# SSD mixer: an even tile's diagonal matmuls queued behind its odd neighbour's, its carried matmuls in one run in another PSUM bank, and a warm-up on a constant

## The chip, the cores and the metric

One core of a Trainium2 chip runs the kernel. A core has five engines with queues of their own: TensorE (PE in the profile; PEld is its loading of the stationary operand, which overlaps with matmuls), VectorE (DVE), ScalarE (ACT), GpSimd (POOL) and SyncE (SP, which here only issues DMAs). Each engine takes its instructions in the order in which they were written into its queue, and waits on semaphores of the others. Matmuls write to PSUM, which has eight banks of 512 fp32 numbers per partition; all else lies in SBUF.

The metric is the time of one execution on the device, in microseconds. Before: a median of 1420.25 over 3 runs (1419.76 to 1420.65).

## The reference

Two layers over 512 tokens of width 1024. Layer 0 mixes tokens with a Mamba-2 SSD, layer 1 with HGRN2; after each comes a squared-ReLU MLP, with layer norms around, and a gated embedding. The change is in layer 0's mixer, at the very start of the kernel, and in one line of layer 1. The SSD cuts the 512 tokens into four chunks of 128, and computes for each head:

```python
cb = jnp.einsum('bclgn,bcsgn->bcgls', cm, bm)
y_diag = jnp.einsum('bcgls,bcgrls,bcsgrp->bclgrp', cb, decay, xdt)
states = jnp.einsum('bclgn,bclgr,bclgrp->bcgrpn', bm, decay_to_end, xdt)
# prev: the states, carried from chunk to chunk with the chunk's decay
y_off = jnp.einsum('bclgn,bcgrpn,bclgr->bclgrp', cm, prev, jnp.exp(a_cs))
y = y_diag + y_off + d_skip * xs        # then times silu(z), an RMS norm, and w_out
```

`y_diag` is what a chunk takes from itself (the diagonal part), `y_off` what it takes from the chunks before (the carried part).

## The kernel before

**Matmuls.** A projection in fp32 is made of three fast matmuls: each operand is split into a high and a low part (`whi`/`wlo` for weights, `b8` for activations), and `mm3` (lines 120 to 122) adds high by high, high by low and low by high into one bank. A weight unit is loaded by SP (`raw`, line 106), its high part is cut by ACT (line 113), and its low part by DVE (line 116). These matmuls are 512 columns wide, and nearly all of the kernel's time. The SSD's small products (lines 676, 703, 715, 745, 751, 777) are plain fp32 matmuls of 128 or 64 columns. The profile counts such an fp32 matmul as two passes, so three of them show as x6, and eight as x16.

**The SSD's loop.** Sixteen tiles of 128 channels (two heads of 64) pass one after another. In step `j` the loop projects tile `j` (`xz`: 48 fast matmuls for x and z, a convolution on DVE, line 644), and works on tile `i = j - 1` in `core`. Per tile, `core` does this:

- four transposes of xs into the bank `pt` (line 703); DVE makes from it `xw` and `xdt` (lines 710 and 711);
- the states: three matmuls into the bank `pm` (line 715), from which DVE forms the carried states `pv` in five instructions (lines 722 to 725), each of which needs the one before;
- the decay matrix `m`, on DVE and ACT (lines 731 to 735);
- the diagonal part: eight matmuls (line 745) whose stationary operand, a head's slice of `xdt`, is 64 columns wide. They write the two halves of the bank `py0`, one head to each;
- the carried part: three matmuls (line 751) into the bank `py1`, one for each of chunks 1 to 3, each with another of the three carried states as an operand;
- the sum of these, in the DVE lines 758 to 761, and then the scaled and split result in `ys` (lines 810 and 811) and its squares (line 766).

After every fourth tile an RMS norm is due (`rms_group`: 16 passes, line 777, whose stationary operand is 64 columns wide as well), and a quarter of the output projection.

**What sets the order.** The kernel's text is not the order on the engines. A scheduler takes the instructions by their dependences, by a priority, and by its own estimates of durations, and writes a fixed order for each engine. `tc.high_priority(offset=n)` moves a block forward in that order, and `behind(ins)` makes a block's instructions on one engine stand after `ins`. The scheduler fills the time between the small products of `core` with the fast matmuls of the next tile's projection. In layer 1's mixer PE's order is written by hand (line 1143); DVE's is still the scheduler's.

**The start.** DVE clears a tile with zeros (line 151), and PE multiplies it four times with itself (line 154) while the first DMAs are on their way; the result is used nowhere. Then come the first projections (lines 593 and 120 to 122), whose operands wait for DMAs (line 162) and for the splits behind them (lines 168 to 173).

**In layer 1**, `out0` (line 899) is a part of the output projection that runs between the small products of the last heads; its result is added to `acc` by DVE (line 911). The same stretch has DVE instructions on the path of PE's small products: lines 965 and 966 write `qd`, which line 991's matmuls read, first for one head and then for the other.

Of the kernel before, what the change touches and what calls it, by code (L numbers as in the profile page):

```python
# [8 lines left out]
F32 = mybir.dt.float32  # L9
# [6 lines left out]
P = 128  # L16
# [28 lines left out]
def trunk(ctx: ExitStack, tc, a):  # L45
# [27 lines left out]

    two = dict(xs=2, sz=2, cv=2, cm=2, cbm=2)
    mlp = dict(r=8, blk=2, sg=2)
    bufs = dict(ssd=dict(two, ss=2), mlp0=mlp, hgrn=dict(two, xs=4, sz=4, cv=4, y=2, pv=2, btok=2, sc=2, scb=2, qd=2), mlp1=mlp)
    phase = []

    def begin(name):
# [67 lines left out]
    acc = mk(accp, [P, NCH, D], "acc")  # L147

    with tc.high_priority(offset=FIRST):
        idle = tmp("sq", [P, T])  # L150
        nc.vector.memset(idle, 0.0)
        ps = bank(psm, "pm")
        for _ in range(4):
            nc.tensor.matmul(ps[:, :256], idle[:, :P], idle[:, :256], start=True, stop=True)  # L154

    x_s = Split(8)
    four = [(mk(whip, [P, 2, T], "whi", F32R), mk(wlop, [P, 2, T], "wlo", F32R)) for _ in range(4)]
# [535 lines left out]
        nc.scalar.activation(sz, ps, AF.Silu)  # L693
        return xs, sz

    def core(j, xs, sz, y, toks, btok, cbm, cm, ss=None):
# [41 lines left out]
        for r in range(2):  # L738
            rs = slice(64 * r, 64 * r + 64)
            nc.scalar.activation(ecs[rs], csb[rs, r, P:], AF.Exp)  # L740
        yd = bank(psy, "py0")
        for c in range(NCH):
            sl = slice(c * P, (c + 1) * P)
            for r in range(2):
                nc.tensor.matmul(  # L745
                    yd[64 * r : 64 * r + 64, sl], xdt[:, 2 * c + r, :], m[:, r, sl], start=True, stop=True
                )
        ri = None if ss is None else rms_group(ss)
        yo = bank(psy, "py1")
        for c in range(1, NCH):  # L750
            nc.tensor.matmul(  # L751
                yo[:, c * P : (c + 1) * P],
                pv[:, c - 1].rearrange("p h q -> p (h q)"),
                cm[:, c * P : (c + 1) * P],
                start=True,
                stop=True,
            )
        nc.vector.scalar_tensor_tensor(y, xs, dskip[:, j : j + 1], yd, ALU.mult, ALU.add)
# [13 lines left out]
    def rms_group(ss):  # L772

        pr = bank(pst, "pt")
        for c in range(NCH):
            for r in range(0, P, 64):
                nc.tensor.matmul(
                    pr[r : r + 64, 64 * c : 64 * c + 64], ss[:, c * P + r : c * P + r + 64], ones_s, start=True, stop=True
                )
# [6 lines left out]
        out_project(a["wso"][4 * g : 4 * g + 4], s, False, *after, scale=ri)  # L786

    pend = None
    ys = None
    bcm = None  # L790
    prep = None
    outs = []
    for j in range(17):
        nbcm = bc_group(j // 4) if j % 4 == 0 and j < 16 else None
        cur = xz(j) if j < 16 else None
        if j == 4:
            nc.sync.dma_start(acc, a["x"])
            for c in range(NCH):
                nc.vector.tensor_scalar(acc[:, c, :], acc[:, c, :], ALPHA, None, ALU.mult)
        if pend is not None:  # L800
            i = j - 1
            if i % 4 == 0:
                ys = Split(4)
                ss = None
                prep = bc_prep(bcm)
            y = tmp("y", [P, T])
            due = bool(outs) and (i % 4 == 1 or i == 15) and i != 13
            ri = core(i, *pend, y, toks, *prep, outs[0][2] if due else None)
            w = snw[:, i : i + 1]
            nc.scalar.activation(ys.h(i % 4), y, AF.Copy, scale=w)  # L810
            nc.vector.scalar_tensor_tensor(ys.l(i % 4), y, w, f32(ys.h(i % 4)), ALU.mult, ALU.subtract)
            ss = sq_sum(y, ss)
# [86 lines left out]
    def out0():  # L899
        for h in range(2):  # L900
            units = [unit(a["who"][2 * h + i]) for i in range(2)]
            for c in range(NCH):
                sl = slice(c * P, (c + 1) * P)
                ps = bank(psj, "pj")
                for k in range(4):
                    hi, lo = units[k // 2]
                    ks = slice((k % 2) * 512, (k % 2 + 1) * 512)
                    mm3(ps, halves[0].h(k, sl), halves[0].l(k, sl), hi[:, ks], lo[:, ks], k == 0, k == 3)
                    yield 0.65
                d = acc[:, c, h * 512 : (h + 1) * 512]  # L910
                nc.vector.scalar_tensor_tensor(d, d, ALPHA, ps, ALU.mult, ALU.add)

    def background():
        yield from qf(0)
# [365 lines left out]
```

## Time and profile before

| | |
|---|---|
| median of 3 runs | 1420.25 us (1419.76 to 1420.65) |
| the profiled execution | 1420.26 us, its span 1418.5 us |
| around the span | 1.76 us |
| DVE, ACT busy | 1057.1 us (75%), 754.1 us (53%) |
| the SSD with its output projection | about the first 390 us of the span |
| layer 1's mixer | about 770 to 1040 us |

The span is one profiled execution from its first to its last instruction. In the timeline a row has its start, its duration, the engine, the line, the operation, output and inputs, and a count of instructions that were merged into it. Matmuls overlap, and their ends are modelled, so what one costs is read from the starts of the rows around it, and not from its duration. In the lists of waits a row has the engine and line that waited, what it waited for, the total, the number of times and the longest.

### The profile page before, as it was taken

Reading aid. Unit: us, or ns where it says so; the run is one execution under the profiler, and the core shown is the slowest. Engines: PE = TensorE matmul, PEld = TensorE weight load, DVE = VectorE, ACT = ScalarE, POOL = GpSimd, SP = SyncE. Lnnn points to the kernel's source line nnn. Section 1 sums busy time; section 2 is a strip of 40 time slices with the busy share of each in tenths; the row PEclk is TensorE's granted clock in tenths of the full one; section 3 lists DMA queues with packets and bytes.
Section 4 is the critical chain, followed back from the end, with each engine's and each line's share of the span. In section 5 each row is a group of like instructions: output and inputs, shape, how many; then the busy total and the mean of one; then the engine's idle time right before and its main releaser. Section 6 shows DMA issues by size and latency. Waiting matters only on the chain.

```text
span 1418.5 us, 20411 instructions
## 1 busy us (share of the span) xinstructions
PE 1412.0 (100%) x8061; PEld 1174.1 (83%) x8061; DVE 1057.1 (75%) x1760; ACT 754.1 (53%) x1134; POOL 1.9 (0%) x12
## 2 busy tenths in 40 slices
PE   9999999999999999999999999999999999999998
PEld 7888888888888888888888888887898888888887
DVE  7988687787877667677986577678785867667873
ACT  6776455563265454545555547655555544544641
POOL 0000000000000000000000000000000000000000
PEclk9999999999999999999999999999999999999999
DMA  8432323223333434344521321222063444434231
GB/s 304 138 129 95 119 90 119 104 101 122 150 133 122 155 130 155 132 154 163 208 90 49 134 90 61 76 91 91 33 250 104 149 148 135 149 134 164 90 119 45
DMA packets 49391, 178.02 MB, mean 126 GB/s; under 512 B 5520, under 2 KB 6288, under 8 KB 49168
## 3 DMA queue, kind: packets, MB, share of 16 engines
q1 hardware_dynamic: 49296, 176.73, 35.8%
q8 instruction: 63, 1.03, 0.3%
q14 instruction: 32, 0.26, 0.1%
HBM read 174.54 MB, written 2.16 MB: 125 GB/s over the span
## 4 chain that ended last, share of the span: by engine, by line
PE 98%; ACT 1%; DVE 1%; issue 0%; DVEq 0%; ACTq 0%
PE pj L120 25%; PE pj L121 25%; PE pj L122 24%; PE py L120 5%; PE py L122 5%; PE py L121 5%; PE py L745 1%; PE pt L239 1%; PE py L751 1%; PE pm L715 1%; PE py L991 1%; PE pt L703 1%; PE py L1117 0%; PE py L1119 0%; PE py L1056 0%; PE pm L154 0%
## 5 line engine op out<-in xcount | busy, mean ns | idle before, releaser
L113 ACT CAST whi<-raw 128x1024 fp32r<-128x1024 f32 x222 | 232.9, 1052 | 326.4 <-PE pj L121 233.1
L120 PE MATMUL pj<-b,whi 128*128 128x512 f32 (+1 forms) x1006 | 383.0, 381 | 0.0
L121 PE MATMUL pj<-b,whi 128*128 128x512 f32 (+1 forms) x1006 | 380.4, 378 | 0.0
L122 PE MATMUL pj<-b,wlo 128*128 128x512 f32 (+1 forms) x1006 | 379.9, 378 | 0.0
L116 DVE TENSOR_TENSOR wlo<-raw,whi 128x1024 fp32r<-128x1024 f32 x222 | 269.6, 1220 | 137.2 <-ACT whi L113 132.6
L120 PEld LDWEIGHTS pj<-b,whi 128*128 128x128 f32 x1006 | 189.4, 188 | 33.5 <-issue 0.3
L122 PEld LDWEIGHTS pj<-b,wlo 128*128 128x128 f32 x1006 | 189.3, 188 | 33.4
L121 PEld LDWEIGHTS pj<-b,whi 128*128 128x128 f32 x1006 | 189.4, 188 | 33.1 <-issue 0.9
L122 PE MATMUL pj<-whi,b 128*128 128x512 f32 x544 | 213.6, 393 | 0.0
L120 PE MATMUL pj<-whi,b 128*128 128x512 f32 x536 | 213.0, 397 | 0.0
L121 PE MATMUL pj<-wlo,b 128*128 128x512 f32 x536 | 210.3, 392 | 0.0
L122 PEld LDWEIGHTS pj<-whi,b 128*128 128x128 f32 x544 | 102.2, 188 | 20.9
L120 PEld LDWEIGHTS pj<-whi,b 128*128 128x128 f32 x536 | 100.8, 188 | 20.2 <-ACT b L1138 0.3
L121 PEld LDWEIGHTS pj<-wlo,b 128*128 128x128 f32 x536 | 100.8, 188 | 19.5
L113 ACT CAST whi<-r 128x1024 fp32r<-128x1024 f32 x72 | 75.7, 1053 | 67.7 <-PE pj L122 38.6
L116 DVE TENSOR_TENSOR wlo<-r,whi 128x1024 fp32r<-128x1024 f32 x72 | 87.6, 1219 | 23.8 <-ACT whi L113 23.2
L122 PE MATMUL py<-whi,b 128*128 128x512 f32 (+1 forms) x250 | 97.0, 388 | 0.0
L121 PE MATMUL py<-wlo,b 128*128 128x512 f32 x224 | 87.2, 389 | 0.0
L120 PE MATMUL py<-whi,b 128*128 128x512 f32 x224 | 87.1, 390 | 0.0
L122 PEld LDWEIGHTS py<-whi,b 128*128 128x128 f32 x250 | 46.9, 188 | 9.6
L644 DVE SCALAR_TENSOR_TENSOR cv<-pj,cst,cv 128x509 f32<-128x509 f32 (+2 forms) x66 | 48.6, 744 | 3.5 <-ACT cv L641 2.8
L120 PEld LDWEIGHTS py<-whi,b 128*128 128x128 f32 x224 | 42.0, 188 | 9.2 <-DVE sg L504 0.3
(310 smaller groups left out, 1864.3 us busy)
## 6 DMA issues: line engine op xcount, KB each, us to landing
raw<-in_w SPq DMA_DIRECT2D x112, 512.0 KB, 3.3
r<-in_w SPq DMA_DIRECT2D x64, 512.0 KB, 3.4
raw<-in_wssd SPq DMA_DIRECT2D x36, 512.0 KB, 3.4
a<-csd SPq DMA_DIRECT2D x16, 512.0 KB, 3.7
raw<-in_wso SPq DMA_DIRECT2D x16, 512.0 KB, 3.2
raw<-in_wg SPq DMA_DIRECT2D x16, 512.0 KB, 3.5
raw<-in_whq SPq DMA_DIRECT2D x16, 512.0 KB, 3.3
raw<-in_whvg SPq DMA_DIRECT2D x14, 512.0 KB, 3.3
```

What stands on the lines that cost most here:

```text
L113: nc.scalar.copy(hi[:, :n], f)
L116: nc.vector.tensor_sub(lo[:, :n], f, f32(hi[:, :n]))
L120: nc.tensor.matmul(out, sh, mh, start=start, stop=False, **kw)
L121: nc.tensor.matmul(out, sh, ml, start=False, stop=False, **kw)
L122: nc.tensor.matmul(out, sl, mh, start=False, stop=stop, **kw)
L239: nc.tensor.transpose(pt[:, j * P : (j + 1) * P], src[:, k * P : (k + 1) * P], ident)
L644: nc.vector.scalar_tensor_tensor(cv[:, d:], ps[:, : T - d], convw[:, i, k : k + 1], cv[:, d:], ALU.mult, ALU.add)
L703: nc.tensor.transpose(pt[:, c * P : (c + 1) * P], xs[:, c * P : (c + 1) * P], ident)
L715: nc.tensor.matmul(pst_[:, c * P : (c + 1) * P], btok[:, c, :], xw[:, c].rearrange("p h q -> p (h q)"), start=True, stop=True)
L745: nc.tensor.matmul(yd[64 * r : 64 * r + 64, sl], xdt[:, 2 * c + r, :], m[:, r, sl], start=True, stop=True)
L751: nc.tensor.matmul(yo[:, c * P : (c + 1) * P], pv[:, c - 1].rearrange("p h q -> p (h q)"), cm[:, c * P : (c + 1) * P], start=True, stop=True,)
L991: nc.tensor.matmul(pcs[r][bs, at : at + n], kk[r][:, ts], qs, start=True, stop=True)
```

## The change

1. **The diagonal part moves.** `core` no longer issues the diagonal matmuls of an even tile. It returns them as a function, and the next, odd tile issues its own eight and, right behind them on PE, the even neighbour's eight. The odd tile's bank is now `py0`, the even one's `py1`. The sums that need them (`finish`, and with it the results' split and squares) wait for both. Tiles 14 and 15, the last two, are not paired. xs, sz, y, xdt and ecs get more buffers (4 or 2), since an even tile's data live longer. An RMS group that is due stands behind the even neighbour's eight.
2. **The carried part** writes the bank `pm`, in which the states were. Its three matmuls go from the last chunk to the first: the first one issued needs the last of the five `pv` instructions, and the other two stand behind it.
3. **The warm-up** at the start reads a constant zero that the program's preamble has written, instead of the tile that DVE cleared; DVE's instruction is gone.
4. **In layer 1**, `out0`'s addition to `acc` gets a lower priority (`offset=-SOON`).

```diff
-    bufs = dict(ssd=dict(two, ss=2), mlp0=mlp, ...
+    bufs = dict(ssd=dict(two, xs=4, sz=4, y=2, xdt=2, ecs=2, ss=2), mlp0=mlp, ...
...
-        idle = tmp("sq", [P, T])
-        nc.vector.memset(idle, 0.0)
+        zero = nc.const_aps.tensor(0.0, (P, 1), F32)
         ps = bank(psm, "pm")
         for _ in range(4):
-            nc.tensor.matmul(ps[:, :256], idle[:, :P], idle[:, :256], start=True, stop=True)
+            nc.tensor.matmul(ps[:, :256], zero.to_broadcast([P, P]), zero.to_broadcast([P, 256]), start=True, stop=True)
...
-        yd = bank(psy, "py0")
-        for c in range(NCH):
-            sl = slice(c * P, (c + 1) * P)
-            for r in range(2):
-                nc.tensor.matmul(
-                    yd[64 * r : 64 * r + 64, sl], xdt[:, 2 * c + r, :], m[:, r, sl], start=True, stop=True
+        yds = []
+
+        def diagonal():
+            yds.append(bank(psy, "py%d" % (1 - j % 2)))
+            for c in range(NCH):
+                sl = slice(c * P, (c + 1) * P)
+                for r in range(2):
+                    mm = nc.tensor.matmul(
+                        yds[0][64 * r : 64 * r + 64, sl], xdt[:, 2 * c + r, :], m[:, r, sl], start=True, stop=True
+                    )
+            return mm
+
+        ri = None
+        if other is not None:
+            mm = diagonal()
+            with behind(mm), tc.high_priority(offset=LEAD):
+                for f in other:
+                    f()
+            with behind(mm):
+                ri = None if ss is None else rms_group(ss)
+        yo = bank(psm, "pm")
+        carried = None
+        for c in range(NCH - 1, 0, -1):
+            with behind(carried):
+                mm = nc.tensor.matmul(
+                    yo[:, c * P : (c + 1) * P],
+                    pv[:, c - 1].rearrange("p h q -> p (h q)"),
+                    cm[:, c * P : (c + 1) * P],
+                    start=True,
+                    stop=True,
                 )
-        ri = None if ss is None else rms_group(ss)
-        yo = bank(psy, "py1")
-        for c in range(1, NCH):
-            nc.tensor.matmul(
...
-        nc.vector.scalar_tensor_tensor(y, xs, dskip[:, j : j + 1], yd, ALU.mult, ALU.add)
+            carried = carried or mm
         nc.vector.tensor_mul(ecs, yo[:, P:], ecs)
-        nc.vector.tensor_add(y[:, P:], y[:, P:], ecs)
-        nc.vector.tensor_mul(y, y, sz)
-        return ri
+
+        def finish():
+            nc.vector.scalar_tensor_tensor(y, xs, dskip[:, j : j + 1], yds[0], ALU.mult, ALU.add)
+            nc.vector.tensor_add(y[:, P:], y[:, P:], ecs)
+            nc.vector.tensor_mul(y, y, sz)
+
+        return ri, diagonal, finish
...
-            ri = core(i, *pend, y, toks, *prep, outs[0][2] if due else None)
...
+            ri, diagonal, finish = core(i, *pend, y, toks, *prep, outs[0][2] if due else None, [f[0] for f in half] if i % 2 or i >= 14 else None)
+            half.append((diagonal, i, finish, y))
+            for _, n, done, y in half if i % 2 or i >= 14 else ():
+                done()
...
+            if i % 2 or i >= 14:
+                half = []
...
-                nc.vector.scalar_tensor_tensor(d, d, ALPHA, ps, ALU.mult, ALU.add)
+                with tc.high_priority(offset=-SOON):
+                    nc.vector.scalar_tensor_tensor(d, d, ALPHA, ps, ALU.mult, ALU.add)
```

What the scheduler makes of it shows in the engines' orders. In them a row has the line, the operation, the output and the inputs, the output's size, and a count; numbers behind a name tell buffers apart. After the change, line 745 is line 747, 751 is 764, 715 is 714, 722 to 725 are 721 to 724, 731 is 730, 758 is 775, 911 is 935, and 965, 966 and 1002 are 989, 990 and 1026.

PE, tile 3 of the SSD, from its states on, before. `pm` holds the states, `py0` the diagonal part, `py1` the carried part, and `pj` is the next tile's projection:

```order
L715 MATMUL pm_156_937<-xw_155_934,btok_64_443 128x128 x3
L745 MATMUL py0_161_963<-b_159_949,xdt_154_933 64x128 x8
L751 MATMUL py1_162_972<-cm_43_344,pv_158_943 128x128 x2
L121 MATMUL pj_164_985<-b8_5_107,whi_166_988 128x512
L122 MATMUL pj_164_985<-b8_5_107,wlo_167_990 128x512
```

The same place after the change:

```order
L714 MATMUL pm_153_918<-xw_152_915,btok_63_441 128x128 x3
L747 MATMUL py0_158_944<-b_156_930,xdt_151_914 64x128 x8
L747 MATMUL py1_159_953<-b_122_735,xdt_117_719 64x128 x8
L121 MATMUL pj_163_983<-b8_6_107,whi_165_986 128x512
L122 MATMUL pj_163_983<-b8_4_105,wlo_166_988 128x512
L120 MATMUL pj_163_983<-b8_4_105,whi_165_986 128x512
```

Tile 2's eight diagonal matmuls (`py1`, of buffers made in tile 2) now follow tile 3's eight. The carried part, before in pieces of two and one, comes as one run of three, seven projection matmuls after the diagonal parts. So it is for all seven pairs: in the whole SSD PE's order had 17 separate runs of line 745 and has 10 of line 747, and the 48 carried matmuls stood in 47 places and stand in 16.

DVE, the chain of `pv` in the same tile before, with the carried part's first reader at the end:

```order
L725 TENSOR_TENSOR pv_158_943<-pm_156_937,pv_158_943 128x128
L116 TENSOR_TENSOR wlo_225_1283<-raw_223_1279,whi_224_1281 128x1024
L724 TENSOR_TENSOR pv_158_943<-pv_158_943,cd_157_941 128x128
L758 SCALAR_TENSOR_TENSOR y_151_925<-xs_108_673,cst_22_167,py0_161_963 128x512
L725 TENSOR_TENSOR pv_158_943<-pm_156_937,pv_158_943 128x128
L731 TENSOR_SCALAR b_213_1225<-a_206_1202,toks_55_402 128x128 x3
L759 TENSOR_TENSOR ecs_160_960<-py1_162_972,ecs_160_960 128x384
```

And after:

```order
L724 TENSOR_TENSOR pv_155_924<-pm_153_918,pv_155_924 128x128
L730 TENSOR_SCALAR b_188_1093<-a_181_1070,toks_54_400 128x128
L723 TENSOR_TENSOR pv_155_924<-pv_155_924,cd_154_922 128x128
L775 SCALAR_TENSOR_TENSOR y_114_711<-xs_81_524,cst_21_165,py1_159_953 128x512
L724 TENSOR_TENSOR pv_155_924<-pm_153_918,pv_155_924 128x128
L776 TENSOR_TENSOR y_114_711<-y_114_711,ecs_123_746 128x384
L775 SCALAR_TENSOR_TENSOR y_148_906<-xs_107_671,cst_21_165,py0_158_944 128x512
L772 TENSOR_TENSOR ecs_157_941<-pm_160_962,ecs_157_941 128x384
```

The weight split (line 116) that stood inside this tile's chain stands ahead of it, and the even neighbour's sum over the diagonal part (`y_114`) is now inside it.

DVE in layer 1, where line 966 releases PE's matmuls of two heads, before:

```order
L1002 TENSOR_TENSOR qd_1335_8468<-qd_1335_8468,y_1357_8594 128x16x8x2
L911 SCALAR_TENSOR_TENSOR acc_2_99<-acc_2_99,pj_1360_8658 128x512
L965 TENSOR_TENSOR qd_1334_8467<-qd_1334_8467,y_1356_8593 128x16x2x4 x2
L965 TENSOR_TENSOR qd_1335_8468<-qd_1335_8468,y_1357_8594 128x16x2x4
L966 TENSOR_TENSOR qd_1334_8467<-qd_1334_8467,y_1356_8593 128x16x8
L965 TENSOR_TENSOR qd_1335_8468<-qd_1335_8468,y_1357_8594 128x16x2x4
L966 TENSOR_TENSOR qd_1335_8468<-qd_1335_8468,y_1357_8594 128x16x8
```

And after:

```order
L1026 TENSOR_TENSOR qd_1334_8466<-qd_1334_8466,y_1356_8592 128x16x8x2
L989 TENSOR_TENSOR qd_1333_8465<-qd_1333_8465,y_1355_8591 128x16x2x4 x2
L989 TENSOR_TENSOR qd_1334_8466<-qd_1334_8466,y_1356_8592 128x16x2x4
L990 TENSOR_TENSOR qd_1333_8465<-qd_1333_8465,y_1355_8591 128x16x8
L989 TENSOR_TENSOR qd_1334_8466<-qd_1334_8466,y_1356_8592 128x16x2x4
L935 SCALAR_TENSOR_TENSOR acc_2_99<-acc_2_99,pj_1359_8656 128x512
L990 TENSOR_TENSOR qd_1334_8466<-qd_1334_8466,y_1356_8592 128x16x8
```

The addition to `acc` has moved from ahead of the first head's last instruction to a place ahead of the second head's.

More of the change, by code (lines that the diff above doesn't have):

```diff
@@ L75, in trunk @@
     mlp = dict(r=8, blk=2, sg=2)
-    bufs = dict(ssd=dict(two, ss=2), mlp0=mlp, hgrn=dict(two, xs=4, sz=4, cv=4, y=2, pv=2, btok=2, sc=2, scb=2, qd=2), mlp1=mlp)
+    bufs = dict(ssd=dict(two, xs=4, sz=4, y=2, xdt=2, ecs=2, ss=2), mlp0=mlp, hgrn=dict(two, xs=4, sz=4, cv=4, y=2, pv=2, btok=2, sc=2, scb=2, qd=2), mlp1=mlp)
     phase = []
@@ L694, in xz, with core @@
         return xs, sz
-    def core(j, xs, sz, y, toks, btok, cbm, cm, ss=None):
+    def core(j, xs, sz, y, toks, btok, cbm, cm, ss=None, other=None):
         dt_tok, w_tok, cs_tok = toks
@@ L740, in core @@
             nc.scalar.activation(ecs[rs], csb[rs, r, P:], AF.Exp)
-        yd = bank(psy, "py0")
-        for c in range(NCH):
-            sl = slice(c * P, (c + 1) * P)
-            for r in range(2):
-                nc.tensor.matmul(
-                    yd[64 * r : 64 * r + 64, sl], xdt[:, 2 * c + r, :], m[:, r, sl], start=True, stop=True
-                )
-        ri = None if ss is None else rms_group(ss)
-        yo = bank(psy, "py1")
-        for c in range(1, NCH):
[L751 to L757, printed above, removed]
```

9 lines of the change are left out of this document (5 added, 4 removed).

## The prediction

> **What bounds the kernel now.** The page's busy times, its granted clock in 40 slices and its chain come first, then the window of the SSD with each engine's busy time (PE, PEld, DVE, ACT, POOL), the granted clock, and the DMAs' share and rate.
>
> ```profile
> PE 1412.0 (100%) x8061; PEld 1174.1 (83%) x8061; DVE 1057.1 (75%) x1760; ACT 754.1 (53%) x1134; POOL 1.9 (0%) x12
> PEclk9999999999999999999999999999999999999999
> PE 98%; ACT 1%; DVE 1%; issue 0%; DVEq 0%; ACTq 0%
> 9.00:350.00 341.00, 340.78 (x1925) 281.98 (x1924) 279.14 (x536) 207.25 (x277) 0.00 (x0) 1.00 0.36 127
> ```
>
> PE is busy for 1412.0 of the span's 1418.5 us, and 98% of the chain is PE. In the SSD it stood still for 0.22 us of 341. So nothing is won by relieving another engine; time is won only where PE's own queue gets shorter, or a wait in it goes. The list of waits has every place where PE itself stood still, and, in its last row, the longest waits of its weight loads for `btok`, which can hold the matmul behind them:
>
> ```profile
> PE pm L154 <- DVE sq L151: 1.5, 1, 1.5
> PE py L991 <- DVE qd L966: 0.9, 1, 0.9
> PE pt L703 <- ACT btok L672: 0.2, 1, 0.2
> PEld pt L703 <- ACT btok L672: 1.5, 4, 0.6
> ```
>
> But "busy" is modelled, so what a piece of PE's queue costs is taken from starts. The timeline of PE in tile 2, and then where an RMS group (line 777) follows a diagonal part:
>
> ```profile
> 72.04 0.40 PE L120 MATMUL pj<-b,whi 128*128 128x512 f32 x1
> 72.27 0.83 PE L715 MATMUL pm<-xw,btok 128*128 128x128 f32 x6
> 72.86 0.48 PE L121 MATMUL pj<-b,whi 128*128 128x512 f32 x1
> 73.17 0.40 PE L122 MATMUL pj<-b,wlo 128*128 128x512 f32 x1
> 73.41 0.39 PE L120 MATMUL pj<-b,whi 128*128 128x512 f32 x1
> 73.73 1.09 PE L745 MATMUL py<-b,xdt 128*64 128x128 f32 x16
> 74.75 0.49 PE L751 MATMUL py<-cm,pv 128*128 128x128 f32 x2
> 75.00 0.48 PE L121 MATMUL pj<-b,whi 128*128 128x512 f32 x1
> 75.31 0.40 PE L122 MATMUL pj<-b,wlo 128*128 128x512 f32 x1
> ...
> 76.00 0.39 PE L122 MATMUL pj<-b,wlo 128*128 128x512 f32 x1
> 76.23 0.39 PE L120 MATMUL pj<-b,whi 128*128 128x512 f32 x1
> 76.46 0.38 PE L751 MATMUL py<-cm,pv 128*128 128x128 f32 x2
> 76.59 0.48 PE L121 MATMUL pj<-b,whi 128*128 128x512 f32 x1
> 76.91 0.40 PE L122 MATMUL pj<-b,wlo 128*128 128x512 f32 x1
> ```
> ```profile
> 128.65 0.82 PE L745 MATMUL py<-b,xdt 128*64 128x128 f32 x12
> 129.30 0.63 PE L777 MATMUL pt<-ones_s,ss 128*64 128x64 f32 x16
> ```
>
> A fast matmul steps every 0.23 us (76.00 to 76.23). What an inserted piece costs is the way from the fast matmul ahead of it to the second one behind it, less two steps (0.46). So the three states' matmuls cost 73.17 - 72.04 - 0.46 = 0.67; one carried matmul 76.91 - 76.23 - 0.46 = 0.22; the diagonal part with a carried one 75.31 - 73.41 - 0.46 = 1.44, and so the diagonal part alone 1.22. But inside a diagonal part, 12 passes take 129.30 - 128.65 = 0.65, 0.054 each, and 16 would be 0.87. The missing 0.35 lies at the two ends, where PE goes from a stationary operand 128 columns wide to one 64 wide and back (73.41 to 73.73 is 0.32 where a step is 0.23; the carried matmul that follows takes 0.25 to the next start, and alone 0.13). At 129.30 the next piece has 64 columns too and goes to another bank, and there is no such gap.
>
> **The change, part by part.**
>
> *The diagonal part of seven even tiles* stands directly behind that of the odd neighbour. It keeps its 16 passes (0.87) and loses its two ends: 7 x (1.22 - 0.87) = 2.4 us off PE's queue, which has no cover. Ends: 0, if the gap belongs to each diagonal part and not to the change of width; 2.5.
>
> *The carried part in one run.* Three single ones cost 3 x 0.22 = 0.66, and three in a run should cost what the states' three cost (same shapes), 0.67. So this is worth 0, with 0.02 per tile, 0.3 in all, either way. Both are 128 wide; there is no end to save.
>
> *Its bank.* In `pm` the carried run waits until DVE has read the states, which its operand `pv` needs anyway, and the next tile's states wait until line 772 has read the carried part; that comes some 30 fast matmuls later (7 us). 0.
>
> *The one wait ahead of the run.* Behind it stands all of PE's queue. The run needs the last `pv`. In tile 3, after the end of the first diagonal part (which frees the buffer that a line 730 among them writes), DVE still has three of line 730, four of lines 723 and 724, and one of line 775. The rows of DVE for the same kinds before:
>
> ```profile
> 98.89 1.22 DVE L116 TENSOR_TENSOR wlo<-raw,whi 128x1024 fp32r<-128x1024 f32 x1
> 100.02 0.29 DVE L724 TENSOR_TENSOR pv<-pv,cd 128x128 f32<-128x128 f32 x1
> 100.22 0.74 DVE L758 SCALAR_TENSOR_TENSOR y<-xs,cst,py 128x512 f32<-128x512 f32 x1
> 100.88 0.28 DVE L725 TENSOR_TENSOR pv<-pm,pv 128x128 f32<-128x128 f32 x1
> ```
>
> A short one holds DVE for 0.20 (100.02 to 100.22), line 758 (now 775) for 0.66 (100.22 to 100.88), the last takes 0.28: 6 x 0.20 + 0.66 + 0.28 = 2.1 us. PE has meanwhile the second diagonal part and seven fast matmuls, 0.87 + 7 x 0.23 = 2.5, and some 0.1 for the change of width. Half a us is left, of which the end of the first diagonal part and two signals take some 0.3. It just fits: I count 0.1 us in all for places that don't, with 0 and 16 x 0.2 = 3.2 as ends (0.2 being an error of one of these short instructions in each tile).
>
> *Waits on `btok`*: 1.5 us of weight loads in four places, of which PE itself shows 0.2. The order has the transposes of a group's first tile four fast matmuls behind the `btok` transposes' run where in one group they were two. I take 0.15 off (0 to 0.4).
>
> *The last two tiles* keep their widths' changes (three runs of diagonal parts before and after); 0, with 0.3 either way from one more or less wait of the size above.
>
> *The start.* The warm-up no longer waits for DVE's clearing.
>
> ```profile
> 0.73 1.28 ACT L172 ACT_TABLE_LOAD   x1 [0.73 <-PEq L1268]
> 0.91 0.48 DVE L151 MEMSET sq<- 128x512 f32 x1 [0.91 <-PEq L1268]
> 1.45 3.78 PE L154 MATMUL pm<-sq 128*128 128x256 f32 x8 [1.45 <-DVE sq L151]
> 4.75 1.34 PE L593 MATMUL py<-b,whi 128*128 128x512 f32 x2
> 5.88 1.06 PE L593 MATMUL pj<-b,whi 128*128 128x512 f32 x2
> 6.74 0.78 PE L593 MATMUL py<-b,whi 128*128 128x512 f32 x2
> 7.36 0.63 PE L593 MATMUL pj<-b,whi 128*128 128x512 f32 x2
> ```
> ```profile
> 4.18 0.43 DVE L168 CAST b<-acc 128x512 fp32r<-128x512 f32 x1 [2.78 <-DMA acc<-in_xw]
> ```
>
> PE could begin where ACT and DVE do, at 0.73 to 0.91 and not at 1.45. The real matmuls cannot: their operand is cast until 4.61, which a DMA sets. They step by 0.43 at first (5.88 to 6.74 for two) and by 0.23 later; the change falls at about 7.1, 5.65 us after PE's first work, which the granted clock, nine tenths or more in the first slice too, doesn't show. If the fast step comes as long after the first work as now, it comes 0.54 to 0.72 earlier, and each us of it wins 1 - 0.23 / 0.43 = 0.47: 0.3 us. The first real matmul stood behind the last warm-up pass (1.45 + 3.78 = 5.23) and now stands behind the cast; that is 0.1 more. Together 0.4 off. The other end: the warm-up now ends at 4.5 to 4.7, so PE may idle for up to half a us before the real work. If that starts the wait anew, the fast step comes at 4.75 + 5.65 = 10.4, 3.3 later, and 3.3 x 0.47 = 1.5 is lost.
>
> [...]
>
> *Layer 1.* PE waits 0.9 us at line 991.
>
> ```profile
> 976.45 0.68 DVE L911 SCALAR_TENSOR_TENSOR acc<-acc,pj 128x512 f32<-128x512 f32 x1
> 977.65 0.28 DVE L966 TENSOR_TENSOR qd<-qd,y 128x128 f32<-128x128 f32 x1
> 978.17 0.29 DVE L966 TENSOR_TENSOR qd<-qd,y 128x128 f32<-128x128 f32 x1
> 978.08 1.13 PE L991 MATMUL py<-qd,cv 128*32 128x56 f32 x64 [0.88 <-DVE qd L966]
> ```
>
> Line 911 moves behind the first head's line 966, so the first head starts 0.6 earlier. But it is still ahead of the second head's, which therefore ends at 978.46 as before, and the second head's matmuls, half of 1.13 behind 978.08, start at about 978.6 in both. What is late next is the same instruction: 0.05 off (0 to 0.6).
>
> Sum, against the profiled execution's 1420.26 (span 1418.5; the median of the runs shown is 1420.25): -2.4 + 0 + 0.1 - 0.15 + 0 - 0.4 - 0.05 = -2.9. I take 1417.4.
>
> **Rivals.**
>
> *A late clock*: all as above, but the pause costs 1.5 where 0.4 was won. 1420.26 - 2.5 + 1.5 = 1419.3. For it: the fast step needed 5.65 us of work without a pause. Against it: the pause is short beside that.
>
> *The diagonal part saves nothing*, because the ends belong to a part and not to a width: 1420.26 - 0.5 = 1419.8. Against it stands 129.30, where two different pieces of the same width follow without a gap.
>
> *The carried run comes late, and the kernel is slower.* It needs the last of five chained DVE instructions where the first single one needed the first; if a weight split (1.22 us) slips into the chain or its own input is late, PE stands still in each tile. By 0.2% slower means 2.9 won and 2.8 lost, 5.7 us in 16 tiles: it decides from 0.36 us per tile past the margin. A split's full 1.22 in half the tiles gives 1420.26 - 2.9 + 9.8 = 1427. For it: the order has a split inside the chain in nine tiles. Against it: it stood there in six before, with PE waiting 0.2 us in all the SSD.
>
> *Some of these waits*, 0.1 in each tile: 1417.4 + 1.6 = 1419.0.
>
> **How the numbers follow.** The sum holds: 0.55, with 1416.6 to 1418.1 as its own range (the small terms' ends, 0.3 to 0.4 each). A late clock: 0.24. Nothing saved: 0.06. Some waits: 0.10. Slower by late runs: 0.05. 0.2% is 2.84 us, about what a measurement of this kernel can tell from no change, and lies at 1417.41, in the middle of the first case: of its 0.55, 0.34 is below (the two terms that I count as losses or as nothing, the chain and the last tiles, are likelier to be better than worse), and with a lucky part of the second, where the window falls well, faster is 0.38. Slower by over 0.2% is 0.04, the rest is 0.58. The range reaches over the late clock and the case of some waits: 1416.2 to 1419.7.
>
> **What would show it.** In the SSD: line 747 as x32, some 2.1 us long to the next start, and the same piece of two tiles shorter by 0.35; no wait of PE at line 764. At the start: line 153 at 0.73 to 0.91, and the step of two fast matmuls going from 0.86 to 0.46 before 7.1 (right) or near 10 (late clock). At line 1015 (991 before) PE's wait split in two, its end unchanged. Wrong would be waits for `pv` at line 764 of over 0.1 us each, or two diagonal parts that still cost 2.4.

## The result, and the profile after

The changed kernel takes 1416.81 us (median of 11 runs, 1415.96 to 1417.90) where the kernel before takes 1420.25 (11 runs beside it): a ratio of 0.9975, 95% interval 0.9967 to 0.9983. That is 3.4 us less. Measured a second time it took 1417.04 where the kernel before took 1420.43 (0.9976, 0.9967 to 0.9986). The forecast was 1417.4, its range 1416.2 to 1419.7. The profiled execution took 1416.50, its span 1414.7, so 3.8 less than the profiled one before.

First the page's busy times and chain after, then the window of the SSD, then PE's own waits and the weight loads' waits that matter here:

```profile
PE 1409.0 (100%) x8061; PEld 1173.2 (83%) x8061; DVE 1056.3 (75%) x1759; ACT 753.8 (53%) x1134; POOL 1.9 (0%) x12
PE 98%; ACT 1%; DVE 1%; issue 0%; DVEq 0%; ACTq 0%
```
```profile
9.00:350.00 341.00, 340.77 (x1937) 283.83 (x1936) 281.95 (x540) 207.25 (x278) 0.00 (x0) 1.00 0.37 129
```
```profile
PE pm L153 <- PEq L1292: 0.8, 1, 0.8
PE py L1015 <- DVE qd L990: 0.7, 2, 0.4
PE pt L702 <- ACT btok L671: 0.2, 1, 0.2
...
PEld pm L764 <- issue: 1.1, 5, 0.4
...
PEld pt L702 <- ACT btok L671: 0.7, 1, 0.7
```

PE is as full as before, with 3.0 us less to do, and gets through 1937 records in the 341 us where it was 1925. There is still no wait of PE itself at line 764, the carried run; but PEld stood idle ahead of its weight loads in five places, 1.1 us in all. The waits of weight loads for `btok` went from 1.5 us in four places to 0.7 in one.

The timeline of PE in tiles 2 and 3: a pair of diagonal parts, and the carried run.

```profile
94.30 0.40 PE L120 MATMUL pj<-b,whi 128*128 128x512 f32 x1
94.53 0.83 PE L714 MATMUL pm<-xw,btok 128*128 128x128 f32 x6
95.30 1.97 PE L747 MATMUL py<-b,xdt 128*64 128x128 f32 x32
97.19 0.50 PE L121 MATMUL pj<-b,whi 128*128 128x512 f32 x1
97.53 0.40 PE L122 MATMUL pj<-b,wlo 128*128 128x512 f32 x1
...
98.70 0.39 PE L121 MATMUL pj<-b,whi 128*128 128x512 f32 x1
98.93 0.83 PE L764 MATMUL pm<-cm,pv 128*128 128x128 f32 x6
99.52 0.47 PE L122 MATMUL pj<-b,wlo 128*128 128x512 f32 x1
99.83 0.39 PE L120 MATMUL pj<-b,whi 128*128 128x512 f32 x1
```

By the prediction's way of reading (from the fast matmul ahead to the second one behind, less two steps), the states with two diagonal parts cost 97.53 - 94.30 - 0.46 = 2.77 us; the forecast's terms give 0.67 + 1.22 + 0.87 = 2.76. The carried run costs 99.83 - 98.70 - 0.46 = 0.67, as forecast.

Where the 3.8 us came from can be read at two marks that both kernels have, the first transposes of xs and the last RMS sums. Before, then after:

```profile
44.38 0.66 PE L703 MATMUL pt<-cst,xs 128*128 128x128 f32 x4 [0.22 <-ACT btok L672]
...
348.99 0.69 PE L777 MATMUL pt<-ones_s,ss 128*64 128x64 f32 x16
```
```profile
43.42 0.66 PE L702 MATMUL pt<-cst,xs 128*128 128x128 f32 x4 [0.23 <-ACT btok L671]
...
345.35 0.69 PE L794 MATMUL pt<-ones_s,ss 128*64 128x64 f32 x16
```

0.96 us lie ahead of the first mark, 2.68 between the two (304.61 against 301.93), and 0.12 behind the last (1418.48 - 348.99 against 1414.72 - 345.35, with the spans to two places). What lies between them, added up over all small pieces of PE's queue by the same reading, with a fast step of 0.227, its median (pieces that touch are split with the price that the smaller one has alone; a step larger by 0.001 moves the row of the carried parts by 0.1 before and by 0.03 after):

| us in PE's queue | before | after | difference | forecast |
|---|---|---|---|---|
| ahead of the first mark (the start) | 44.38 | 43.42 | -0.96 | -0.4 |
| states, diagonal parts, RMS sums | 32.35 | 29.89 | -2.46 | -2.4 |
| carried parts | 11.12 | 11.14 | +0.02 | 0 + 0.1 |
| transposes of xs | 7.84 | 7.60 | -0.24 | -0.15 |
| all else between the marks | | | 0.00 | 0 |
| behind the last mark (layer 1 and the rest) | 1069.49 | 1069.37 | -0.12 | -0.05 |
| sum | | | -3.76 | -2.9 |

The profile of the second measurement repeats the middle of this and not its ends: 301.86 us between the marks (2.75 less than before), but 1069.71 behind the last, which is 0.22 more than before.

### The profile page after: what moved, and what is told of

Same layout as the page of the kernel before. It is cut to its first block, busy times and chain, and to the rows that moved or that the text cites. A ratio compares the mean times of both kernels' runs of the same rounds, so it can differ in the third digit from the quotient of the medians.

```text
span 1414.7 us, 20411 instructions
## 1 busy us (share of the span) xinstructions
PE 1409.0 (100%) x8061; PEld 1173.2 (83%) x8061; DVE 1056.3 (75%) x1759; ACT 753.8 (53%) x1134; POOL 1.9 (0%) x12
## 4 chain that ended last, share of the span: by engine, by line
PE 98%; ACT 1%; DVE 1%; issue 0%; DVEq 0%; ACTq 0%
PE pj L120 25%; PE pj L121 25%; PE pj L122 25%; PE py L120 5%; PE py L122 5%; PE py L121 5%; PE py L747 1%; PE pt L238 1%; PE pm L764 1%; PE pm L714 1%; PE py L1015 1%; PE pt L702 1%; PE py L1141 0%; PE py L1143 0%; PE py L1080 0%; PE pm L153 0%
```

## The experiments

### The pairing undone

```diff
-            ri, diagonal, finish = core(..., [f[0] for f in half] if i % 2 or i >= 14 else None)
+            ri, diagonal, finish = core(..., [])
...
-            for _, n, done, y in half if i % 2 or i >= 14 else ():
+            for _, n, done, y in half:
...
-            if i % 2 or i >= 14:
-                half = []
+            half = []
```

> The changed kernel with the pairing alone undone: every tile issues its own diagonal part behind its own states, so PE's queue has 18 runs of narrow matmuls where the changed kernel has 10 and a pair in one piece; the carried run, its bank and the start stay as changed. Theory (each entry into and exit from 64 wide stationary operands costs 0.35 us): 1416.8 + 7 x 0.35 = 1419.2, a piece of states and diagonal part about 1.89 us longer than the fast matmuls alone in every tile. Rival (the gain of 3.4 us came from the start, layer 1 and lost waits, and a diagonal part costs the same wherever it stands): 1416.8, not different from the changed kernel by more than 0.3.

Measured: 1420.05 us, 0.9998 of the kernel before (0.9989 to 1.0007). Nearly all of the gain is gone, so the rival (the gain lies elsewhere) falls. The same place of tile 3:

```profile
96.13 0.40 PE L120 MATMUL pj<-b,whi 128*128 128x512 f32 x1
96.37 0.83 PE L714 MATMUL pm<-xw,btok 128*128 128x128 f32 x6
97.13 1.09 PE L747 MATMUL py<-b,xdt 128*64 128x128 f32 x16
98.15 0.50 PE L121 MATMUL pj<-b,whi 128*128 128x512 f32 x1
98.49 0.39 PE L122 MATMUL pj<-b,wlo 128*128 128x512 f32 x1
```

98.49 - 96.13 - 0.46 = 1.90, as expected. Two tiles then cost 2 x 1.90 = 3.80 where the changed kernel has 2.77 for the pair and 0.68 for the even tile's states, 3.45: 0.35 per pair. Over the fourteen paired tiles the trace has 2.42 us more than the changed kernel, 7 x 0.346. The time rose by 3.2, 0.8 more than expected: between the marks this kernel takes 305.12, 3.19 more than the changed one. The 0.77 beside the 2.42 is a net of other shifts in the order (transposes of xs that come late in three groups, +0.5; the last two tiles, +0.3; other small gaps, +0.3; a carried run that is never late, -0.34). So undoing one part of the change isn't the same as taking its term off the sum.

### A narrow and a wide matmul between the two diagonal parts

Both kernels put one small fp32 matmul between the diagonal parts of each of the seven pairs. Its result is used nowhere. They differ in the width of its stationary operand alone, and with it in the number of rows that it writes.

```diff
             mm = diagonal()
+            if other:
+                gap = bank(pst, "pt")
+                with behind(mm), tc.high_priority(offset=LEAD):
+                    mm = nc.tensor.matmul(gap[:64, :32], cm[:, :64], cm[:, :32], start=True, stop=True)
```
In the wide one the last line is:

```diff
+                    mm = nc.tensor.matmul(gap[:128, :32], cm[:, :128], cm[:, :32], start=True, stop=True)
```

> The changed kernel with one more small fp32 matmul (64 x 32 out, its result used nowhere) between the two diagonal parts of seven pairs; its stationary operand has 64 columns, like those around it. Theory (the width's change costs): only the passes of the extra matmul, 7 x 0.1 or less; at most 1417.5. Rival (any other piece between two diagonal parts costs, whatever its width): as much as the wide twin, within 0.5 us.

> The same small matmul with a stationary operand of 128 columns (128 x 32 out, its result used nowhere). Theory (the width's change costs): an exit and an entry more in seven places, 7 x 0.35 = 2.4 us more than the narrow twin, about 1419.5 to 1420. Rival (the gap belongs to the part, not to the width): within 0.5 us of the narrow twin.

Measured on one chip: 1418.15 us with the narrow one (0.9988 of the kernel before, 0.9978 to 0.9997) and 1420.75 with the wide one (1.0003, 0.9994 to 1.0012), 2.6 apart where the theory of widths expected 2.4 and its rival 0.5 at most. PE's timeline at the pair of tiles 2 and 3, narrow and then wide (line 758 is the added matmul):

```profile
94.68 0.40 PE L120 MATMUL pj<-b,whi 128*128 128x512 f32 x1
...
98.02 0.40 PE L122 MATMUL pj<-b,wlo 128*128 128x512 f32 x1
```
```profile
94.54 0.39 PE L120 MATMUL pj<-b,whi 128*128 128x512 f32 x1
...
95.53 1.09 PE L747 MATMUL py<-b,xdt 128*64 128x128 f32 x16
96.55 0.41 PE L758 MATMUL pt<-cm 128*128 128x32 f32 x2
96.89 1.09 PE L747 MATMUL py<-b,xdt 128*64 128x128 f32 x16
...
98.25 0.39 PE L122 MATMUL pj<-b,wlo 128*128 128x512 f32 x1
```

The piece costs 98.02 - 94.68 - 0.46 = 2.88 with the narrow matmul, 0.11 more than without, and 98.25 - 94.54 - 0.46 = 3.25 with the wide one. Both have two passes, and the 0.37 between them are what it costs PE to leave the narrow width and come back. Seven times this is 2.6. A little of the 0.37 may be the wide operand's longer load (0.19 us for 128 columns against 0.14 for 64 in PEld's rows of the changed kernel); the pairing undone, which adds no matmul, gives 0.35 without it. Both kernels are slower than expected (at most 1417.5, and 1419.5 to 1420): 7 x 0.11 is 0.77 over the changed kernel, and in both the carried run came 0.22 late in three tiles, where the changed kernel has one such place.

What happens at a change of width can be read from PEld's starts, in the changed kernel's pair of tiles 2 and 3. Within the narrow run a load starts some 0.1 us ahead of its matmul, under the matmuls before it (96.88 for the matmul at 96.98). On the way in the first narrow load starts at 95.29, only with its matmul, 0.20 us after the start of the states' last pass (95.09); on the way out the first wide load starts at 97.19, again with its matmul, 0.20 us after the start of the last narrow one (96.99). The loads of the new width aren't hidden there. The wide matmul adds one more way out and back in (96.55 and 96.89 in its kernel).

Why these loads come late the rows don't show, since the ends of matmuls are modelled. The price of the way there and back is 0.35 to 0.37 us here, between operands of 128 and 64 columns in fp32.

### The start: the old one back, and the new one alone

In the first, the changed kernel has the warm-up of before; in the second, the kernel before has the new warm-up and nothing else of the change.

```diff
-        zero = nc.const_aps.tensor(0.0, (P, 1), F32)
+        idle = tmp("sq", [P, T])
+        nc.vector.memset(idle, 0.0)
```

> The changed kernel with the warm-up as it was before (on a tile that DVE clears first); all else as changed. Theory (the fast step comes as long after PE's first work as before, so the earlier start won 0.4 by the sum, and 0.95 by the two profiled executions): 1417.2 to 1417.8, the step of two fast matmuls going from 0.86 to 0.46 near 7.1 us again. Rival (the start is free): 1416.8.

> The kernel before with the new warm-up alone. Theory: 1420.25 less 0.4 to 0.95, so 1419.3 to 1419.85, ratio 0.9993 to 0.9997; the fast step by 6 us. Rival (the pause of PE between the warm-up and the real work starts the clock's wait anew): 1421.75. Rival (the start explains most of the gain of 3.4): below 1418.5.

Measured: 1417.38 with the old start (0.9977 of the kernel before, 0.9969 to 0.9986), so 0.3 to 0.6 above the changed kernel's 1417.04 and 1416.81; and 1420.03 with the new start alone, 0.5 below the kernel before beside it (0.9997, 0.9988 to 1.0006). Both agree with the forecast's 0.4, and neither interval tells 0.4 from nothing. The fast step came at 6.29 us with the old start and at 6.90 with the new one alone, where 7.1 and 6 at the latest were expected; both were missed. That the start made most of the gain is excluded, and so is a loss of 1.5 with four multiplies. The 0.96 us between the two profiled executions is more than the medians have; the next runs show why.

### Fewer and more warm-up multiplies, and the changed kernel again

The diff is that for two multiplies; others had five and, twice, three, and one was the changed kernel itself.

```diff
-        for _ in range(4):
+        for _ in range(2):
```

> The changed kernel with two warm-up multiplies instead of four: PE's warm-up ends near 2.7 us and PE stands still for 1.5 to 2 us before its first real matmul. Theory one (the clock's wait counts from the first work, and a pause of 2 us does not matter): the fast step as early as with four, near 5.5, time 1416.8 within 0.3. Rival, the late clock of the prediction (a pause starts the wait anew): the fast step near 4.55 + 4.7 = 9.3 us, time 1416.8 + 3.8 x 0.47 = 1418.6.

> The changed kernel with five warm-up multiplies: PE has no pause, but the last pass ends near 5.4 us and holds the first real matmul back by up to 0.9 at the slow step. Theory (the pause after four is harmless): 1416.8 plus 0.3 to 0.9 for the late first matmul, fast step near 5.5. Rival (the pause after four costs something): below 1416.8.

> The changed kernel with three warm-up multiplies instead of four: PE stands still for about 1.1 us ahead of its first real matmul. Theory (a long pause starts the clock's wait anew, as with two multiplies, where the fast step came 3.9 us after the pause): fast step near 8.6 us, time like that with two, some 0.6 above the changed kernel. Rival (a pause of 1 us is still harmless): fast step between 3.7 and 6.8 us, time as the changed kernel's within 0.3.

> Three warm-up multiplies once more, since the times of that kernel fell in two groups (three at 1416.3 to 1416.6, eight at 1418.1 to 1419.3) and the profiled execution belongs to the first, with the fast step there before PE's pause and kept over it. Theory (where the fast step has not come before the pause of 1 us, the pause starts the wait anew): a profiled execution of the second group shows the slow step of 0.43 until 8 to 10.5 us, and one of the first the fast step by 5 us. Rival (the two groups have another cause, later in the kernel): the start looks the same in both, and the 2 us lie elsewhere.

> The changed kernel again, on the chip of the two runs that follow. If the moment at which the fast step comes differs from execution to execution and not from program to program, its own profile has it anywhere from 2.9 to 6.0 us after PE's first work (the bounds of nine profiles so far), where its first profile had it 4.6 after; if it belongs to the program, again at 4.6. The time: 0.9975 of the kernel before, as measured, within 0.0008.

| multiplies | median us | ratio to before | PE's pause ahead of the real work in the profile | fast step from |
|---|---|---|---|---|
| 4 (changed kernel, two profiles) | 1416.81, 1417.04 | 0.9975, 0.9976 | below 0.1; 0.3 | 5.48; 5.17 |
| 5 | 1417.31 | 0.9981 (0.9971 to 0.9990) | 0 | 5.54 |
| 3 (two profiles) | 1418.86, 1418.30 | 0.9985, 0.9985 | 1.00; 1.10 | 4.67 or earlier; 10.38 |
| 2 | 1417.95 | 0.9984 (0.9975 to 0.9993) | 1.95 | 8.68 |

With four multiplies, PE's timeline in the first us:

```profile
0.77 3.75 PE L153 MATMUL pm<-const-float32-0.0 128*128 128x256 f32 x8 [0.77 <-PEq L1292]
4.55 1.09 PE L592 MATMUL py<-b,whi 128*128 128x512 f32 x2
5.48 0.63 PE L592 MATMUL pj<-b,whi 128*128 128x512 f32 x2
5.95 0.63 PE L592 MATMUL py<-b,whi 128*128 128x512 f32 x2
```

With three, in the first profile and then in the second:

```profile
4.67 0.70 PE L592 MATMUL py<-b,whi 128*128 128x512 f32 x2 [1.00 <-DVE b L167]
5.21 0.62 PE L592 MATMUL pj<-b,whi 128*128 128x512 f32 x2
```
```profile
4.77 1.19 PE L592 MATMUL py<-b,whi 128*128 128x512 f32 x2 [1.10 <-DVE b L167]
5.76 1.05 PE L592 MATMUL pj<-b,whi 128*128 128x512 f32 x2
...
9.17 1.05 PE L592 MATMUL pj<-b,wlo 128*128 128x512 f32 x2
10.02 0.52 PE L120 MATMUL py<-b,whi 128*128 128x512 f32 x1
10.38 0.40 PE L121 MATMUL py<-b,whi 128*128 128x512 f32 x1
```

One program, two executions: in one the fast step was there at the first real matmul, behind a pause of 1.00 us; in the other it was not, and came 5.6 us after the pause. The first took 1416.31 and the second 1419.21. The times of this kernel fall into two groups with nothing between, 6 of 19 at 1416.3 to 1416.8 and 13 at 1418.1 to 1419.3. The matmul of line 121 that starts at 10.38 in the second starts at 7.72 in the first, which is 2.66 of the 2.90 us between the two executions.

Whether the fast step came before the pause in the first execution, as the last expectation but one says, or within it, these rows can't show: the warm-up's starts, up to the last at 3.04, step by 0.43 in both. The kernel with the wide matmul has the clear case: there the warm-up's last pass starts 0.31 behind the one before it, at 3.77 (its eight passes take 3.38 us, the changed kernel's 3.75), and the real work steps fast from its start at 4.74 (two matmuls in 0.54, and then in 0.46), over a pause of 0.59.

So the forecast's rival of a late clock is seen in two profiles: where the fast step had not come before the pause, it came 5.6 us after one of 1.10 here, and 3.9 us after one of 1.95 with two multiplies, as though the wait had begun anew. That it came at 10.4 us, where the prediction put it, is luck, since with two multiplies it came at 8.68. With four multiplies, no pause ahead of the fast step was over 0.3 us, and no profile shows it put off.

Of the expectations for three multiplies the first was missed in the time by both its sides: 1418.86 is 1.8 to 2.1 above the changed kernel, not 0.6 and not 0.3, since the time is that of two groups. The second was met: the slow step lasted until 10.38 in the execution of the slow group.

That left the spread within one program. The moment of the fast step, in the eleven profiles without a long pause, lies 3.0 to 6.1 us after PE's first work: 5.7 and 4.8 with the old start; 3.0 and 4.1 at the latest, then 4.4, 4.5, 4.7, 5.1, 5.3 and 6.1 with the new start, whose instructions are the same in these eight; and 4.8 with five multiplies. (The expectations put the moment some 0.1 earlier.) The changed kernel's two profiles alone, 4.7 and 4.4, would not have told this. The values spread over 3.1 us. By the two steps (0.43 and 0.23, so 0.47 per us) this is worth an estimated 3.1 x 0.47 = 1.5 us of time, most of what one kernel's runs spread by (1415.96 to 1417.90); run by run that isn't shown, since each kernel has one profile or two.

The expectation for two multiplies (1418.6 if the pause counts, 1416.8 if not) was met by the first in the trace (fast step from 8.68, 3.9 us after the pause) and lies between them in the time. Five multiplies bring nothing that these runs can tell from four.

### The last two tiles paired as well

```diff
-            ... [f[0] for f in half] if i % 2 or i >= 14 else None)
+            ... [f[0] for f in half] if i % 2 else None)
...
-            for _, n, done, y in half if i % 2 or i >= 14 else ():
+            for _, n, done, y in half if i % 2 else ():
...
-            if i % 2 or i >= 14:
+            if i % 2:
```

> The changed kernel with the last two tiles paired like the others: tile 14's diagonal part is queued behind tile 15's too. One more entry and exit of the narrow width goes. Theory: 0.35 less than the changed kernel, 1416.45; and in the end of the SSD the six carried matmuls of tile 14 and 15 may wait for the last pv and give some of it back (0 to 0.35). Rival (no width cost): 1416.8 or more, since tile 14's y comes later, close to the group's end where the sum of squares waits for it: up to 1 us lost.

Measured: 1417.70 us (0.9982, 0.9973 to 0.9991), so not faster than the changed kernel (0.9975), and slower by the medians. PE's queue in these tiles is shorter by the 0.35; but the last RMS sums, which now stand earlier in PE's queue, wait for `ss`. PE, and DVE ahead of it:

```profile
337.74 0.69 PE L794 MATMUL pt<-ones_s,ss 128*64 128x64 f32 x16 [0.95 <-DVE ss L786]
```
```profile
333.90 2.52 DVE L116 TENSOR_TENSOR wlo<-raw,whi 128x1024 fp32r<-128x1024 f32 x2
336.34 0.75 DVE L832 SCALAR_TENSOR_TENSOR b<-y,cst,b 128x512 fp32r<-128x512 f32 x1
337.01 0.68 DVE L786 TENSOR_TENSOR ss<-ss,sq 128x512 f32<-128x512 f32 x1
```

The next kernel kept this pairing and held the sums back to where the changed kernel has them (`newest` holds the last matmul that `mm3` has issued):

```diff
-    ssd_out(g, s, rms_group(ss), *after)
+    with behind(newest[0]):
+        ri = rms_group(ss)
+    ssd_out(g, s, ri, *after)
```

> The last two tiles paired as in the run that did so, and the last group's RMS sums held behind the last matmul of the output projection ahead of them, where the changed kernel has them. Theory (the pairing saves its 0.35 there too, and the loss of 0.9 came from the sums, which stood in PE's queue ahead of their operand): no wait of PE at the last RMS sums, and PE's queue from the first transposes of xw to the last RMS sums 0.46 shorter than in the changed kernel (0.35 and 0.11), 301.93 - 0.46 = 301.47 us; the time 1416.3. Rival (the pairing itself costs in the last group): the way is 301.9 or longer.

Measured: 1418.33 us (0.9987, 0.9978 to 0.9995), no better, and 303.42 us between the two marks, where the theory had 301.47 and the rival 301.9 or longer. The wait at the sums is gone, and another stands in its place, at a fast matmul that needs a bank of `pj` (lines count two more here):

```profile
337.44 2.72 DVE L260 SCALAR_TENSOR_TENSOR acc<-pj,ri,acc 128x512 f32<-128x512 f32 x4
...
338.24 0.50 PE L122 MATMUL pj<-whi,b 128*128 128x512 f32 x1 [1.61 <-DVE acc L260]
```

DVE has both tiles' sums, splits and squares to do in one stretch, with two weight splits (2.5 us) among them, and reads the projection's banks only after them. With two tiles ended at once and no third one behind to fill PE, DVE sets the pace. So the theory's 0.35 is there (the small pieces of PE's queue between the marks sum to 0.35 less than in the changed kernel), and more is lost than it saves: the changed kernel, which leaves tiles 14 and 15 unpaired, has the lowest median of all that ran.

## Why the prediction was right

**The diagonal part.** -2.4 forecast, -2.46 found between the marks and 2.42 by undoing it; and the reason, the change of width and not the part, is shown by the narrow and the wide matmul. The rival "the diagonal part saves nothing" falls. Of its signs, "some 2.1 us long to the next start" reads 1.89 (95.30 to 97.19), because the ends' cost lies in part ahead of the first start and behind the next (the states' last pass starts 0.20 ahead of 95.30, where their step is 0.11; 97.19 to 97.53 is 0.34, where a fast step is 0.23).

**The carried part, its bank and the wait ahead of it.** 0 and +0.1 were forecast; sixteen runs cost 11.14 us, against 11.12 for 48 single ones before. Two errors cancel in this, which is luck: a single one had cost 0.23 and not the 0.22 that the prediction took, while sixteen runs on time would cost 10.85 (0.678 each), some 0.25 less than the single ones; but the runs come late by 0.3 in all, not by 0.1. Most of that lateness (0.21) lies in one place, tile 12:

```profile
297.41 0.39 PE L121 MATMUL pj<-b,whi 128*128 128x512 f32 x1
297.78 0.91 PE L764 MATMUL pm<-cm,pv 128*128 128x128 f32 x6
```
```profile
296.21 1.23 DVE L116 TENSOR_TENSOR wlo<-raw,whi 128x1024 fp32r<-128x1024 f32 x1 [0.33 <-ACT whi L113]
297.35 0.28 DVE L724 TENSOR_TENSOR pv<-pm,pv 128x128 f32<-128x128 f32 x1
```

The last `pv` came behind a weight split, the very mechanism of the rival that ended slower. It cost 0.21 there and 0.05 or less in the other places, where that rival needed 0.36 per tile past the margin. "It just fits" held, with a margin near zero (the 0.3 in it for the end of a diagonal part and two signals was an estimate; from the end of the DVE instruction that PE waits for to PE's start layer 1's rows below have 0.15 and 0.16, 973.66 to 973.81 and 974.66 to 974.82): a small matmul more between the diagonal parts was enough to make three tiles late by 0.22 where there had been one.

**Waits on `btok`.** -0.15 forecast, -0.24 found, 0.19 of it in one place: the transposes at 292.37 before cost 0.63, those at 289.44 after cost 0.45. PE's own list of waits had no row for it.

**The last two tiles.** 0 forecast; they are part of the rows above, and no term of their own can be told from them.

**The start.** -0.4 forecast; -0.3 to -0.6 by the medians. The -0.96 of the two profiles has chance in it, since the moment of the fast step alone moves a time by up to 1.5, by the estimate above. The prediction took the fast step as a fixed 5.65 us after the first work, from the one profile that it had; it is not fixed (3.0 to 6.1 in eleven profiles). This step agrees with the medians in size, which can't be told from nothing, and was wrong in its mechanism; a single profile could not show that.

**Layer 1.** -0.05 forecast. What it brought in time isn't shown: behind the last mark the changed kernel's two profiles have 0.12 less and 0.22 more than the one before. But PE's wait fell from 0.9 to 0.7 and is split in two, as forecast. DVE's rows, and then PE's:

```profile
973.38 0.28 DVE L990 TENSOR_TENSOR qd<-qd,y 128x128 f32<-128x128 f32 x1
...
973.79 0.68 DVE L935 SCALAR_TENSOR_TENSOR acc<-acc,pj 128x512 f32<-128x512 f32 x1
974.38 0.28 DVE L990 TENSOR_TENSOR qd<-qd,y 128x128 f32<-128x128 f32 x1
```
```profile
973.81 0.60 PE L1015 MATMUL py<-qd,cv 128*32 128x56 f32 x32 [0.30 <-DVE qd L990]
974.82 0.60 PE L1015 MATMUL py<-qd,cv 128*32 128x56 f32 x32 [0.40 <-DVE qd L990]
```

The addition still stands ahead of the second head's `qd`, and so PE waits for it a second time.

**The sum.** The terms of the SSD made -2.45 in the forecast and -2.68 and -2.75 in the two profiles: the diagonal part as forecast, the others a little better. With a start of -0.3 to -0.6 this is -3.0 to -3.4, and the medians have -3.4. The range, 1416.2 to 1419.7, was wide enough for the late clock as well, so that a time within it says little by itself; 1416.81 also lies within the range of the first case alone (1416.6 to 1418.1), near its lower end. The chance was given more to a change too small to tell (0.58) than to a gain over 0.2% (0.38); the interval of 0.17% to 0.33% leaves both open, with the middle, 0.25%, on the side of the gain. A part of the 0.38 is put on a window of the clock that "falls well"; no run shows such a window, and what the runs showed in its place is the spread of the fast step's moment over 3.1 us.

## What to carry to other kernels

Where PE's queue is the bound, count how often it changes between stationary operands of different widths: each way there and back between 128 and 64 columns cost 0.35 to 0.37 us here, and queueing equal widths together takes it off without removing any work. The cover for that is the time until someone needs the result that was put off: in the middle of the SSD the next tile's projection gave it, at its end DVE was late at once, by 0.95 and 1.61 us. And a warm-up should reach the real work without a pause: with three multiplies (a pause of 1.00 and 1.10 us in the two profiles) 13 of 19 executions took some 2 us longer than the other 6.

## What the runs showed of the hardware

- The moment of PE's fast step varied from 3.0 to 6.1 us after PE's first work, in executions with the same start. The profile's granted clock is 1.00 for the window from 0 to 9 us in the six profiles where it was taken (before, after, the pairing undone, the narrow and the wide matmul, the last two tiles paired), and its mean is 0.999 or 1.000 in all fourteen; only the steps of the matmuls (0.43, then 0.23) show it.
- A pause of 0.59 us behind the fast step left it as it was (the wide matmul's kernel); ahead of it, the step came 5.6 us after a pause of 1.10 (three multiplies) and 3.9 us after one of 1.95 (two).
- In the changed kernel's tile 12 the carried run's first weight load starts at 297.75, 0.12 us after the end of the last `pv` and 0.37 us after the load ahead of it had ended. It cost PE 0.21 us without a row in PE's list of waits: at 297.78 only the start is late.
- At a change between stationary operands of 128 and 64 columns the first weight load starts with its matmul, 0.20 us after the start of the matmul ahead (95.29 and 97.19 in the changed kernel); within the narrow run a load starts some 0.1 us ahead.
- The two heads' narrow matmuls, which write the two halves of a bank's partitions, start 0.007 us apart (95.564 and 95.571 in the changed kernel), and such pairs follow each other every 0.11 us, the step of one matmul of 128 columns (the states' passes, 94.87 to 94.98). So two narrow matmuls together took the time of one of 128 columns.
